# A transformer layer's opening, its gates and its v projections: reordering work around a full TensorE

## The chip, the cores and the metric

One of the cores of a Trainium2 chip runs the whole kernel in one launch. The metric is the device time of one execution in microseconds (us), lower is better. The engines that matter here are TensorE (PE, with its weight loads PEld), VectorE (DVE), ScalarE (ACT), GpSimd (POOL) and SyncE (SP), which issues nearly all transfers.

## The reference, cut to what matters

One layer over 512 tokens of width 1024: a first feed-forward block, a mixer of a chunked mLSTM and a forgetting attention, and a second feed-forward block, each behind an RMS norm that is scaled and shifted by columns computed from a condition vector `c`.

```python
mod = jax.nn.silu(c) @ w_ada + b_ada
sh1, sc1, g1, sh2, sc2, g2, sh3, sc3, g3 = ...
u = rms_norm(x, ffn1_norm_g) * (1 + sc1) + sh1
x = x + 0.5 * g1 * swiglu(u, ffn1_w_in, ffn1_w_out)

u = rms_norm(x, mix_norm_g) * (1 + sc2) + sh2
z = u @ w_mix + b_mix            # q_m k_m v_m o_m i_m f_m q_f k_f v_f f_f g_a g_b
qk_m = jax.nn.silu(causal_conv(jnp.concatenate([q_m, k_m], axis=-1), conv_w, conv_b))
h_m = mlstm_chunkwise(q_m, k_m, v_m, i_m, f_m)
y_a = jax.nn.sigmoid(o_m) * rms_norm(h_m, mlstm_norm_g)
y_b = forgetting_attention(q_f, k_f, v_f, f_f, fox_q_norm_g, fox_k_norm_g)   # 16 heads of 64
merged = jax.nn.sigmoid(g_a) * (y_a @ w_branch_a) + jax.nn.sigmoid(g_b) * (y_b @ w_branch_b)
x = x + g2 * (merged @ w_out)

u = rms_norm(x, ffn2_norm_g) * (1 + sc3) + sh3
x = x + 0.5 * g3 * swiglu(u, ffn2_w_in, ffn2_w_out)
```

All data is float32. The width is 8 blocks of 128 channels, the tokens are 4 blocks of 128.

## The kernel before, in words

**Precision.** Every product is made from rounded high halves and their remainders: a weight is loaded into a `raw` tile (three buffers), `split` (lines 94 to 104) makes its high half `wh` on ScalarE (line 101) and the remainder `wl` on VectorE (line 103), four buffers each. `mm3` (lines 124 to 128) then issues three matmuls, high by high, high by low, low by high. A stationary block is 128x128; the moving side has up to 512 columns. PSUM holds eight banks of 512 columns, four with the tag `g` (`gbank`) and four with the tag `t` (`tbank`).

**Order.** Instructions that are wrapped in `pin` keep the order of the text on their engine. The others are put in order when the kernel is built, by a planner that takes, on each engine, the ready instruction that is first in the text, with its own estimates of when something is ready. On the chip each engine works through its queue in order and waits on semaphores.

**Opening stage** (`start`, lines 693 to 847). The eight channel blocks k of the normalised, scaled input `u` are made one after the other, and each is used at once in 18 matmuls (line 826: three products, six banks). Ahead of block n's use stand: four transposes of the normalised x (`turn(n)`, line 731), the two columns of scale and shift, which VectorE multiplies and adds up from `w_ada` (`mod_first`, `mod`, lines 744 to 752) and TensorE sums over the partitions (`sums(n)`, line 767), two ScalarE instructions on these columns (lines 771, 772), and `uh[n]` and its full value `uf` (lines 773, 775). The low half is a VectorE subtraction (line 777). Block 0's columns come from TensorE directly (`mod0`, line 742). Identity transposes into an unused bank (`fill`, line 726) stand where TensorE waits. In the loop over k, `i` counts the 18 matmuls: before, block 1's transposes are split (two ahead of the loop, two at `i == 7`), its sums stand behind the block after `fill(4)`, and later blocks have transposes at `i == 7` and sums at `i == 12`.

**End of the first FFN** (`end`, lines 1315 to 1396, all pinned). The last banks Z, Y, X, W of the output product are closed, scaled (`scaled`, line 597) and added onto x (`onto`, line 600); x is squared and summed (`x_sq`, line 228). `xnorm` (line 241) turns the sums into a factor per token (`rsqrt`, line 136, a chain of tiny VectorE instructions) and scales x; `norm_turn` transposes (line 295); `u_part` (line 270) makes `u` for half of the tokens. The four first weights of the mixer are split here: `hi(m)` (line 1326) on ScalarE, the function that it returns (line 1328) on VectorE, `lo1`, `lo2`, `lo3` for m = 1, 2, 3. `first(h)` (lines 1380 to 1390) multiplies them with half h of the tokens into four banks `pp[0..3]`, 256 columns at a time.

**Convolutions and gates** (lines 1415 to 1425). `qk_conv(m)` (line 912) takes a bank: a bias copy on ScalarE (line 917), which frees the bank, one and three VectorE instructions (lines 919, 921), Silu (922) and a split (925, 926). `gates` (line 850) projects 280 columns (v of the first four attention heads and the scalar gates) for all tokens in three chunks of weights, 96 matmuls of 280 columns, adds biases (lines 861 to 863), transposes the gates (line 880), and runs a serial chain of Abs, Exp, Ln, scans and Exp (lines 884 to 898). Then channels m = 4 to 7 are projected, one bank and 24 matmuls of 512 columns each.

**Attention heads** (`fox_qkv`, line 1039, and the loop of lines 1462 to 1480). Heads come in four groups g of four. `fox_qkv(g)` projects q and k (512 columns), normalises them, then projects v (256 columns; for g = 0 it is read back from where `gates` put it) and evicts it (`donev`). It is a generator, and so is `gate(m, i)`, a projection of 24 matmuls: the loop over the 16 heads advances them in small steps between the steps of the heads, so that TensorE has work while VectorE and ScalarE run the softmax. `with_gates(gen, n)` appends n gates.

**Ahead of the second FFN** (lines 1515 to 1525) the same `xnorm`, `norm_turn` and `norm_u` (line 299) run twice.

Of the kernel before, what the change touches and what calls it, by code (L numbers as in the profile page):

```python
# [29 lines left out]
BIG = 1e30  # L30
RSQ = (0.2740822732448578, 0.31394892930984497, 0.37500056624412537, 0.4999983012676239, 1.0)

# [14 lines left out]
class Layer:  # L47
# [87 lines left out]

    def rsqrt(self, v, n, pin=lambda i: i):

        nc, sp = self.nc, self.sp
        y = sp.tile([P, n], F32, name=self.nm("rq"), tag=f"rq{n}", bufs=4)
        t = sp.tile([P, n], F32, name=self.nm("rt"), tag=f"rt{n}", bufs=2)  # L140
# [12 lines left out]
        pin(V.scalar_tensor_tensor(y, t, RSQ[4], y, op0=ADD, op1=MUL))  # L153
        return y
# [86 lines left out]
    def xnorm(self, hf, pool):  # L241

        nc, sp = self.nc, self.sp
        v = sp.tile([P, 2], F32, name=self.nm("v"), tag="v", bufs=2)
        s2 = self.ss[:, 2 * hf:2 * hf + 2, :]
        self.pin(nc.vector.tensor_scalar(v, s2[:, :, 0], 1.0 / D, EPS, op0=MUL, op1=ADD))
        self.pin(nc.vector.scalar_tensor_tensor(v, s2[:, :, 1], 1.0 / D, v, op0=MUL, op1=ADD))
        r = self.rsqrt(v, 2, self.pin)
        xn = []
        for i in range(2):  # L250
            x = self.x[2 * hf + i]
            d = self.xn_tiles(pool)
            self.pin(nc.vector.tensor_scalar(d[0], x[0], r[:, i:i + 1], None, op0=MUL))
# [439 lines left out]
    def start(self, st, tp):  # L693
# [16 lines left out]
        def chain(hf):  # L710
            v = sp.tile([P, 2], F32, name=self.nm("v"), tag="v", bufs=2)
            s2 = self.ss[:, 2 * hf:2 * hf + 2, :]
            pin(nc.vector.tensor_scalar(v, s2[:, :, 0], 1.0 / D, EPS, op0=MUL, op1=ADD))
            pin(nc.vector.scalar_tensor_tensor(v, s2[:, :, 1], 1.0 / D, v, op0=MUL, op1=ADD))
            return self.rsqrt(v, 2, pin)
        def norm(tb, h, dve=False):
# [97 lines left out]
        for k in range(NK):  # L814
# [5 lines left out]
            for i, (p, b) in enumerate((p, b) for p in range(3) for b in range(2 * NJ0)):  # L820
                if n < NK and i == 7:
                    turn(n, range(NT) if k else (2, 3))
                if n < NK and k and i == 12:
                    sums(n)
                s = slice(b // 2 * P, (b // 2 + 1) * P)
                pin(nc.tensor.matmul(acc_ps[b], (wl if p == 1 else wh)[:, b % 2, s], self.ul[k] if p == 2 else self.uh[k],  # L826
                                     start=k == 0 and p == 0, stop=k == NK - 1 and p == 2))
# [211 lines left out]
    def fox_qkv(self, g, ip):  # L1039
# [25 lines left out]
        for tb in range(NT):  # L1065
            t3 = tok[tb].rearrange("p (h d) -> p h d", h=8)
            nc.vector.tensor_tensor(t3, t3, r[:, tb * 8:(tb + 1) * 8].unsqueeze(2).to_broadcast([P, 8, 64]), op=MUL)
        bv = self.bias_bcast([(VF + o, 256)], ip) if g else None
        vt = ip.tile([P, NT, 4, P], F32R, name=self.nm("fvt"), tag="vm", bufs=3)
        def donev(tb, ps):  # L1070
            f = ip.tile([P, 256], F32, name=self.nm("vg"), tag="t2", bufs=3)
            if g:
                nc.vector.tensor_tensor(f, ps[:, :256], bv[:, :256], op=ADD)
            else:
                nc.sync.dma_start(f, self.v0_d[tb])
            f4 = f.rearrange("p (h d) -> p h d", h=4)
            nc.scalar.activation(vt[:, tb, :, 0:64], f4, AF.Copy)
            nc.vector.tensor_tensor(vt[:, tb, :, 64:P], f4, vt[:, tb, :, 0:64], op=SUB)
        def mkv(ch):
            def make():  # L1080
                sh = [P, 4, 256]
                r = self.raw(sh, [(lambda t: t, w[ch * 512:(ch + 1) * 512, VF + o:VF + o + 256]
                                   .rearrange("(k p) n -> p k n", p=P))])
                wh, wl = self.split(r, sh)
                return wh, wl, 4 * ch, 4
# [188 lines left out]
    def run(self):  # L1274
# [10 lines left out]
        with tc.tile_pool(name="f1t", bufs=1) as tp:  # L1285
# [5 lines left out]
            with tc.tile_pool(name="f1h", bufs=1) as hp:  # L1291
# [23 lines left out]
                def end(close, scaled, onto):  # L1315
# [110 lines left out]
        with tc.tile_pool(name="att", bufs=1) as ip:  # L1426
# [35 lines left out]
            for n in range(18):  # L1462
                if n % 4 == 0 and n < 16:
                    advance(fill, 99)
                    g = n // 4
                    fill = with_gates(self.fox_qkv(g + 1, ip), 4 if g else 2) if g < 3 else (s for m in range(NK) for s in self.y_a(m, yp, ip))
                last = n >= 12
# [111 lines left out]
```

## Time and profile before

| | |
|---|---|
| median of three runs | 1333.39 us (1333.33 to 1336.34) |
| the profiled execution | 1333.93 us, span 1332.2 us |
| instructions in the span | 18008 |
| busy, share of the span | PE 98%, PEld 82%, DVE 73%, ACT 47%, POOL 3% |
| granted TensorE clock | 1.0 |
| DMA | 254.21 MB, mean 191 GB/s |

Times in rows are us from the span's start. A row of the timeline has start, duration, engine, line, operation, output and inputs, shape, count and, in brackets, how long the engine had been idle before and what ended that. Rows with a count above 1 are merged. A row of the chain has start, duration, engine, output and line. A matmul's duration is its latency; the next one starts earlier.

### The profile page before, as it was taken

Reading aid. Unit: us, or ns where it says so; the run is one execution under the profiler, and the core shown is the slowest. Engines: PE = TensorE matmul, PEld = TensorE weight load, DVE = VectorE, ACT = ScalarE, POOL = GpSimd, SP = SyncE. Lnnn points to the kernel's source line nnn. Section 1 sums busy time; section 2 is a strip of 40 time slices with the busy share of each in tenths; the row PEclk is TensorE's granted clock in tenths of the full one; section 3 lists DMA queues with packets and bytes.
Section 4 is the critical chain, followed back from the end, with each engine's and each line's share of the span. In section 5 each row is a group of like instructions: output and inputs, shape, how many; then the busy total and the mean of one; then the engine's idle time right before and its main releaser. Section 6 shows DMA issues by size and latency. Waiting matters only on the chain.

```text
span 1332.2 us, 18008 instructions
## 1 busy us (share of the span) xinstructions
PE 1311.0 (98%) x6428; PEld 1098.2 (82%) x6428; DVE 966.3 (73%) x1776; ACT 625.0 (47%) x1038; POOL 42.4 (3%) x65
## 2 busy tenths in 40 slices
PE   7999999999999999999999999999999999999998
PEld 6788888878788888888888788778788888888886
DVE  7877777477788687887877778777477656635777
ACT  5533323365476655566666666334253223223742
POOL 1000000000010101000000000003010000000000
PEclk9999999999999999999999999999999999999999
DMA  9999978365835334534252636777529877534574
GB/s 291 276 321 312 317 269 284 113 182 182 280 112 144 108 101 133 159 101 117 65 155 52 181 97 190 217 248 234 163 71 334 282 248 265 201 105 134 172 267 149
DMA packets 205514, 254.21 MB, mean 191 GB/s; under 512 B 15008, under 2 KB 148800, under 8 KB 205424
## 3 DMA queue, kind: packets, MB, share of 16 engines
q1 hardware_dynamic: 205040, 252.98, 60.6%
q8 instruction: 51, 0.84, 0.3%
q14 instruction: 39, 0.32, 0.1%
q0 software_dynamic: 320, 0.06, 0.0%
q10 hardware_dynamic: 64, 0.02, 0.0%
HBM read 217.28 MB, written 35.72 MB: 190 GB/s over the span
## 4 chain that ended last, share of the span: by engine, by line
PE 85%; DVE 7%; DMA 3%; ACT 3%; issue 1%; POOL 0%; ACTq 0%; SPq 0%; DVEq 0%; POOLq 0%
PE g L128 22%; PE g L127 22%; PE g L126 22%; PE t L127 3%; PE t L128 3%; PE t L126 3%; PE g L826 2%; DVE wl L103 2%; PE t L1200 1%; PE t L1170 1%; DMA raw<-in_ffn_w_out_dram 1%; ACT wh L101 1%; PE t L1141 1%; PE t L826 1%; PE t L1142 1%
## 5 line engine op out<-in xcount | busy, mean ns | idle before, releaser
L101 ACT ACTIVATE wh<-raw 128x1024 fp32r<-128x1024 f32 (+2 forms) x250 | 253.8, 1018 | 379.2 <-PE g L127 115.0
L103 DVE TENSOR_TENSOR wl<-raw,wh 128x1024 fp32r<-128x1024 f32 (+2 forms) x250 | 293.4, 1175 | 186.9 <-ACT wh L101 155.6
L127 PE MATMUL g<-ul,wh 128*128 128x512 f32 (+1 forms) x912 | 348.1, 383 | 0.6 <-DVE ul L267 0.3
L126 PE MATMUL g<-uh,wh 128*128 128x512 f32 (+1 forms) x912 | 348.2, 384 | 0.2 <-ACT wh L101 0.2
L128 PE MATMUL g<-uh,wl 128*128 128x512 f32 (+1 forms) x912 | 347.8, 382 | 0.0
L127 PEld LDWEIGHTS g<-ul,wh 128*128 128x128 f32 x912 | 171.3, 188 | 34.0 <-POOL ul L267 1.1
L128 PEld LDWEIGHTS g<-uh,wl 128*128 128x128 f32 x912 | 171.3, 188 | 33.3
L126 PEld LDWEIGHTS g<-uh,wh 128*128 128x128 f32 x912 | 170.8, 188 | 33.0 <-issue 0.6
L126 PE MATMUL g<-wh,uh 128*128 128x512 f32 (+1 forms) x288 | 103.0, 358 | 0.0
L128 PE MATMUL g<-wh,ul 128*128 128x512 f32 (+1 forms) x288 | 102.2, 355 | 0.0
L127 PE MATMUL g<-wl,uh 128*128 128x512 f32 (+1 forms) x288 | 102.0, 354 | 0.0
L325 DVE SCALAR_TENSOR_TENSOR acc<-raw,ccol,acc 128x512 f32<-128x512 f32 (+1 forms) x70 | 66.7, 973 | 30.6 <-DMA raw<-in_w_ada_dram 30.4
L127 PE MATMUL t<-wl,A 128*128 128x512 f32 x176 | 69.2, 393 | 1.1 <-DVE wl L103 1.1
L126 PE MATMUL t<-wh,A 128*128 128x512 f32 x176 | 69.3, 394 | 0.0
L126 PEld LDWEIGHTS g<-wh,uh 128*128 128x128 f32 x288 | 54.3, 189 | 7.7 <-DVE tk L1047 0.5
L128 PEld LDWEIGHTS g<-wh,ul 128*128 128x128 f32 x288 | 54.3, 188 | 7.6
L127 PEld LDWEIGHTS g<-wl,uh 128*128 128x128 f32 x288 | 54.3, 189 | 7.3
L128 PE MATMUL g<-yh,wl 128*128 128x512 f32 x128 | 50.5, 394 | 1.3 <-DVE wl L103 1.3
L127 PE MATMUL g<-yl,wh 128*128 128x512 f32 x128 | 50.2, 393 | 0.0
L126 PE MATMUL g<-yh,wh 128*128 128x512 f32 x128 | 49.9, 390 | 0.0
L455 ACT ACTIVATE A<-E 128x768 fp32r<-128x768 f32 x22 | 18.6, 846 | 55.1 <-DVE E L454 51.0
L1152 ACT ACTIVATE S<-S,mn 128x128 f32<-128x128 f32 (+1 forms) x64 | 35.6, 557 | 17.9 <-DVE mn L1144 9.3
(347 smaller groups left out, 2192.3 us busy)
## 6 DMA issues: line engine op xcount, KB each, us to landing
raw<-in_ffn_w_in_dram SPq DMA_DIRECT2D x82, 512.0 KB
raw<-in_w_ada_dram SPq DMA_DIRECT2D x56, 512.0 KB
raw<-in_w_mix_dram SPq DMA_DIRECT2D x46, 512.0 KB
sa<-in_ffn_w_out_dram SPq DMA_DIRECT2D x22, 512.0 KB
sb<-in_ffn_w_out_dram SPq DMA_DIRECT2D x44, 256.0 KB
ws<-sa SPq DMA_DIRECT2D x22, 512.0 KB
ws<-sb SPq DMA_DIRECT2D x44, 256.0 KB
raw<-ws SPq DMA_DIRECT2D x44, 256.0 KB
```

What stands on the lines that cost most here:

```text
L101: nc.scalar.activation(hi, src, AF.Copy)
L103: self.last_lo = nc.vector.tensor_tensor(lo, src, hi, op=SUB)
L126: pin(mm(ps, lh, rh, start=start, stop=False))
L127: pin(mm(ps, lh, rl, start=False, stop=False))
L128: self.last_mm = pin(mm(ps, ll, rh, start=False, stop=stop))
L325: nc.vector.scalar_tensor_tensor(a, r[:, s], c, a, op0=MUL, op1=ADD)
L455: nc.scalar.activation(A1[:, 0:3, :], E[:, 0:3, :], AF.Copy)
L826: pin(nc.tensor.matmul(acc_ps[b], (wl if p == 1 else wh)[:, b % 2, s], self.ul[k] if p == 2 else self.uh[k], start=k == 0 and p == 0, stop ...
L1141: nc.tensor.matmul(ps[:, :w], q[:, s], k[:, :w], start=True, stop=False)
L1142: nc.tensor.matmul(ps[:, :w], q[:, s], kl[:, :w], start=False, stop=True)
L1152: nc.scalar.activation(S[:, ws], S[:, ws], AF.Exp, scale=-1.0, bias=m, accum_out=sm[:, qb:qb + 1])
L1170: tr = lambda b, c, qb, kb: nc.tensor.transpose(b[:, c:c + P], S[:, P_OFF[qb] + kb * P:P_OFF[qb] + (kb + 1) * P], self.ident)
```

## The change

Six edits.

1. `rsqrt` has 8 VectorE instructions instead of 10 (one for the first guess, the polynomial in two quadratic factors), and the variance ahead of it in the norms over the width takes one instead of two; so 9 instead of 12 there.
2. Opening stage: block 0's two groups of `mod0` matmuls follow each other and its four transposes come behind them; block 1's four transposes all stand at `i == 7` and its sums at `i == 16`, without the fill; later blocks have their sums and right behind them their transposes at `i == 10`.
3. End of the first FFN: `lo2` and `lo3` are made in halves, their second halves after `onto(2, 1, ...)`; one `onto(2, 0, ...)` moves behind `u[7]`.
4. `first(1)` goes over all eight k for channels 0 and 1, then for 2 and 3; `first(0)` stays at k = 0 to 3 and 4 to 7.
5. `gates` stands ahead of the four convolutions in the text.
6. v of head groups 2 and 3 is projected in one product of 512 columns in `fox_qkv(2)`; `fox_qkv(3)` has q and k alone. The numbers of gates behind groups 1, 2, 3 are 2, 2, 6 instead of 2, 4, 4.

```diff
-    def rsqrt(self, v, n, pin=lambda i: i):
+    def rsqrt(self, v, n, pin=lambda i: i, gain=1.0):
...
-        pin(V.tensor_scalar(y.bitcast(I32), v.bitcast(I32), 1, None, op0=ALU.logical_shift_right))
-        pin(V.tensor_scalar(y.bitcast(I32), y.bitcast(I32), -1, 0x5F3759DF, op0=MUL, op1=ADD))
+        s = (gain * RSQ_LEAD) ** 0.25
+        (a0, b0), (a1, b1) = [(a * s, b * s * s) for a, b in RSQ_QUADS]
+        pin(V.tensor_scalar(y.bitcast(I32), v.bitcast(I32), -0.5, 0x5F3759DF, op0=MUL, op1=ADD))
 
         pin(V.tensor_tensor(t, y, y, op=MUL))
-        pin(V.tensor_tensor(t, t, v, op=MUL))
-        pin(V.tensor_scalar(d, t, -1.0, 1.0, op0=MUL, op1=ADD))
-        pin(V.tensor_scalar(t, d, RSQ[0], RSQ[1], op0=MUL, op1=ADD))
-        pin(V.tensor_tensor(t, t, d, op=MUL))
-        pin(V.scalar_tensor_tensor(t, t, RSQ[2], d, op0=ADD, op1=MUL))
-        pin(V.scalar_tensor_tensor(t, t, RSQ[3], d, op0=ADD, op1=MUL))
-        pin(V.scalar_tensor_tensor(y, t, RSQ[4], y, op0=ADD, op1=MUL))
+        pin(V.scalar_tensor_tensor(d, t, -s, v, op0=MUL, op1=MUL))
+        pin(V.tensor_scalar(d, d, s, None, op0=ADD))
+        pin(V.scalar_tensor_tensor(t, d, a0, d, op0=ADD, op1=MUL))
+        pin(V.scalar_tensor_tensor(q, d, a1, d, op0=ADD, op1=MUL))
+        pin(V.scalar_tensor_tensor(y, t, b0, y, op0=ADD, op1=MUL))
+        pin(V.scalar_tensor_tensor(y, q, b1, y, op0=ADD, op1=MUL))
...
-        self.pin(nc.vector.tensor_scalar(v, s2[:, :, 0], 1.0 / D, EPS, op0=MUL, op1=ADD))
-        self.pin(nc.vector.scalar_tensor_tensor(v, s2[:, :, 1], 1.0 / D, v, op0=MUL, op1=ADD))
-        r = self.rsqrt(v, 2, self.pin)
+        self.pin(nc.vector.scalar_tensor_tensor(v, s2[:, :, 0], D * EPS, s2[:, :, 1], op0=ADD, op1=ADD))
+        r = self.rsqrt(v, 2, self.pin, D ** 0.5)
...
         mod0(0)
-        turn(0, (0, 1))
-        turn(1, (0, 1))
         mod0(1)
-        turn(0, (2, 3))
+        turn(0, range(NT))
...
-                if n < NK and i == 7:
-                    turn(n, range(NT) if k else (2, 3))
-                if n < NK and k and i == 12:
+                if n < NK and k == 0 and i == 7:
+                    turn(n, range(NT))
+                if n < NK and i == (10 if k else 16):
                     sums(n)
+                    if k:
+                        turn(n, range(NT))
...
             if n < NK:
-                if k == 0:
-                    fill(4)
-                    sums(n)
                 u_hi(n)
...
-        bv = self.bias_bcast([(VF + o, 256)], ip) if g else None
-        vt = ip.tile([P, NT, 4, P], F32R, name=self.nm("fvt"), tag="vm", bufs=3)
+        if g == 3:
+            self.fx[g] = tok, self.fx[g]
+            return
+        gs = ((0,), (1,), (2, 3))[g]
+        n = len(gs) * 256
+        bv = self.bias_bcast([(VF + o, n)], ip) if g else None
+        vts = [ip.tile([P, NT, 4, P], F32R, name=self.nm("fvt"), tag="vm", bufs=3) for _ in gs]
         def donev(tb, ps):
...
-            f4 = f.rearrange("p (h d) -> p h d", h=4)
-            nc.scalar.activation(vt[:, tb, :, 0:64], f4, AF.Copy)
-            nc.vector.tensor_tensor(vt[:, tb, :, 64:P], f4, vt[:, tb, :, 0:64], op=SUB)
+            for i, vt in enumerate(vts):
+                f4 = f[:, i * 256:(i + 1) * 256].rearrange("p (h d) -> p h d", h=4)
+                nc.scalar.activation(vt[:, tb, :, 0:64], f4, AF.Copy)
+                nc.vector.tensor_tensor(vt[:, tb, :, 64:P], f4, vt[:, tb, :, 0:64], op=SUB)
...
-        self.fx[g] = (tok, vt)
+        self.fx[g] = (tok, vts[0])
+        if len(gs) > 1:
+            self.fx[3] = vts[1]
         if g:
-            yield from self.u_gemm_tokens([mkv(c) for c in range(2)], 256, donev)
+            yield from self.u_gemm_tokens([mkv(c) for c in range(2 * len(gs))], n, donev)
...
                     part(2, 3)
-                    lo2()
                     u[2]()
                     u[3]()
+                    lo2(0, 4)
                     w1 = scaled(W[1], 0)
-                    lo3()
+                    lo3(0, 4)
                     part(4, 5)
                     u[4]()
                     u[5]()
                     onto(2, 1, tx[0, 1])
-                    onto(2, 0, tx[0, 0])
+                    lo2(4, NK)
+                    lo3(4, NK)
                     part(6, 7)
                     u[6]()
                     u[7]()
+                    onto(2, 0, tx[0, 0])
...
-                        for ks in (range(4), range(4, NK)):
+                        for ks in ((range(NK),) if h else (range(4), range(4, NK))):
...
+            columns = self.gates(mp, yp)
             for m in range(4):
                 self.qk_conv(m, self.pp[m], yp, mp)
-            columns = self.gates(mp, yp)
...
-                    fill = with_gates(self.fox_qkv(g + 1, ip), 4 if g else 2) if g < 3 else ...
+                    fill = with_gates(self.fox_qkv(g + 1, ip), (2, 2, 6)[g]) if g < 3 else ...
```

More of the change, by code (lines that the diff above doesn't have):

```diff
@@ L30 @@
 BIG = 1e30
-RSQ = (0.2740822732448578, 0.31394892930984497, 0.37500056624412537, 0.4999983012676239, 1.0)
+RSQ_LEAD = 0.2740822732448578
+RSQ_QUADS = ((-1.0965162378196741, 1.8032570710297795), (2.2419713071789813, 2.0233052502305482))
 QM, KM, VM, OM, IG, FG, QF, KF, VF, FFG, GA, GB = (
@@ L134, in tbank @@
         return self.pt.tile(list(shape), F32, name=self.nm("t"), tag="t")
-    def rsqrt(self, v, n, pin=lambda i: i):
+    def rsqrt(self, v, n, pin=lambda i: i, gain=1.0):
         nc, sp = self.nc, self.sp
         y = sp.tile([P, n], F32, name=self.nm("rq"), tag=f"rq{n}", bufs=4)
-        t = sp.tile([P, n], F32, name=self.nm("rt"), tag=f"rt{n}", bufs=2)
+        t, q = [sp.tile([P, n], F32, name=self.nm("rt"), tag=f"rt{n}", bufs=2) for _ in range(2)]
         d = sp.tile([P, n], F32, name=self.nm("rd"), tag=f"rd{n}", bufs=2)
         V = nc.vector
-        pin(V.tensor_scalar(y.bitcast(I32), v.bitcast(I32), 1, None, op0=ALU.logical_shift_right))
-        pin(V.tensor_scalar(y.bitcast(I32), y.bitcast(I32), -1, 0x5F3759DF, op0=MUL, op1=ADD))
+        s = (gain * RSQ_LEAD) ** 0.25
+        (a0, b0), (a1, b1) = [(a * s, b * s * s) for a, b in RSQ_QUADS]
+        pin(V.tensor_scalar(y.bitcast(I32), v.bitcast(I32), -0.5, 0x5F3759DF, op0=MUL, op1=ADD))
         pin(V.tensor_tensor(t, y, y, op=MUL))
-        pin(V.tensor_tensor(t, t, v, op=MUL))
-        pin(V.tensor_scalar(d, t, -1.0, 1.0, op0=MUL, op1=ADD))
-        pin(V.tensor_scalar(t, d, RSQ[0], RSQ[1], op0=MUL, op1=ADD))
-        pin(V.tensor_tensor(t, t, d, op=MUL))
-        pin(V.scalar_tensor_tensor(t, t, RSQ[2], d, op0=ADD, op1=MUL))
-        pin(V.scalar_tensor_tensor(t, t, RSQ[3], d, op0=ADD, op1=MUL))
-        pin(V.scalar_tensor_tensor(y, t, RSQ[4], y, op0=ADD, op1=MUL))
+        pin(V.scalar_tensor_tensor(d, t, -s, v, op0=MUL, op1=MUL))
[4 more added lines that the diff above has]
+        pin(V.scalar_tensor_tensor(y, q, b1, y, op0=ADD, op1=MUL))
         return y
@@ L712, in chain @@
             s2 = self.ss[:, 2 * hf:2 * hf + 2, :]
-            pin(nc.vector.tensor_scalar(v, s2[:, :, 0], 1.0 / D, EPS, op0=MUL, op1=ADD))
-            pin(nc.vector.scalar_tensor_tensor(v, s2[:, :, 1], 1.0 / D, v, op0=MUL, op1=ADD))
-            return self.rsqrt(v, 2, pin)
+            pin(nc.vector.scalar_tensor_tensor(v, s2[:, :, 0], D * EPS, s2[:, :, 1], op0=ADD, op1=ADD))
+            return self.rsqrt(v, 2, pin, D ** 0.5)
         def norm(tb, h, dve=False):
@@ L1078, in donev @@
-            nc.vector.tensor_tensor(vt[:, tb, :, 64:P], f4, vt[:, tb, :, 0:64], op=SUB)
+            for i, vt in enumerate(vts):
+                f4 = f[:, i * 256:(i + 1) * 256].rearrange("p (h d) -> p h d", h=4)
+                nc.scalar.activation(vt[:, tb, :, 0:64], f4, AF.Copy)
+                nc.vector.tensor_tensor(vt[:, tb, :, 64:P], f4, vt[:, tb, :, 0:64], op=SUB)
         def mkv(ch):
             def make():
-                sh = [P, 4, 256]
-                r = self.raw(sh, [(lambda t: t, w[ch * 512:(ch + 1) * 512, VF + o:VF + o + 256]
+                k = 8 // (2 * len(gs))
+                sh = [P, k, n]
+                r = self.raw(sh, [(lambda t: t, w[ch * k * P:(ch + 1) * k * P, VF + o:VF + o + n]
@@ L1465, in run @@
                     g = n // 4
-                    fill = with_gates(self.fox_qkv(g + 1, ip), 4 if g else 2) if g < 3 else (s for m in range(NK) for s in self.y_a(m, yp, ip))
+                    fill = with_gates(self.fox_qkv(g + 1, ip), (2, 2, 6)[g]) if g < 3 else (s for m in range(NK) for s in self.y_a(m, yp, ip))
                 last = n >= 12
```

6 lines of the change are left out of this document (3 added, 3 removed).

## The prediction

> **What bounds the kernel now.** I read the page's engine line and its chain first, then the busy time by stretches, then the timelines of the stages that the diff touches.
>
> ```profile
> PE 1311.0 (98%) x6428; PEld 1098.2 (82%) x6428; DVE 966.3 (73%) x1776; ACT 625.0 (47%) x1038; POOL 42.4 (3%) x65
> ...
> PE 85%; DVE 7%; DMA 3%; ACT 3%; issue 1%; POOL 0%; ACTq 0%; SPq 0%; DVEq 0%; POOLq 0%
> ```
>
> ```profile
> 300.00:400.00 100.00, 98.57 (x509) 82.67 (x508) 77.75 (x123) 57.01 (x88) 5.21 (x8) 1.00 0.60 191
> 400.00:500.00 100.00, 97.24 (x527) 84.53 (x526) 77.07 (x158) 59.02 (x108) 5.66 (x17) 1.00 0.42 118
> ```
>
> TensorE is the bound: 98% busy, 85% of the chain. So an edit pays only where it takes matmul work away or closes a hole on TensorE; the columns above are span, then PE, PEld, DVE, ACT, POOL busy. The stretch 400:500 holds one hole (2.76 us), 300:400 has 1.43 us. A busy PE still hides waits shorter than a matmul's latency, so I judge by starts, not by busy time. Two pitches are needed:
>
> ```profile
> 59.43 0.39 PE L127 MATMUL g<-ul,wh 128*128 128x512 f32 x1
> ...
> 64.22 0.39 PE L127 MATMUL g<-ul,wh 128*128 128x512 f32 x1
> ```
>
> ```profile
> 642.15 0.28 PE L127 MATMUL g<-wl,uh 128*128 128x256 f32 x1
> ...
> 645.14 0.29 PE L128 MATMUL g<-wh,ul 128*128 128x256 f32 x1
> ```
>
> From the first row to the last are 21 steps in one fence and 25 in the other: 0.2281 us for a 512-column matmul, 0.1196 us for 256 columns, back to back.
>
> **Part A, opening stage.** Timeline, then the chain of waits:
>
> ```profile
> 16.57 0.35 DVE L747 TENSOR_SCALAR ac<-ar,ccol 128x256 f32<-128x256 f32 x1 [0.33 <-DMA ar<-in_w_ada_dram]
> ...
> 19.00 2.04 DVE L752 SCALAR_TENSOR_TENSOR ac<-ar,ccol,ac 128x256 f32<-128x256 f32 x4
> ...
> 23.57 1.20 PE L826 MATMUL g<-uh,wh 128*128 128x512 f32 x4 [1.41 <-ACT uh L773]
> ...
> 25.29 1.00 DVE L752 SCALAR_TENSOR_TENSOR ac<-ar,ccol,ac 128x256 f32<-128x256 f32 x2
> ...
> 30.57 1.00 DVE L752 SCALAR_TENSOR_TENSOR ac<-ar,ccol,ac 128x256 f32<-128x256 f32 x2
> ```
>
> ```profile
> 21.82 0.36 PE t L767 x4
> ...
> 25.45 0.44 PE t L731 x4
> ...
> 27.04 0.34 PE t L767 x4
> 27.38 1.05 PE g L826 x4
> ...
> 28.89 1.09 PE g L826 x4
> ...
> 54.98 1.09 PE g L826 x4
> ```
>
> Block 0: the sums of k=1 stood after the whole block and four filling transposes; now they stand two matmuls before its end. Their input is complete at 19.00+2.04 = 21.04; its start at 16.57 waits for a DMA, so the shorter rsqrt and the regrouped transposes of block 0 can't move it. Sums then run 21.1 to 21.45 instead of 21.82 to 22.18, and block 1 starts 0.73 us earlier. The fill goes; it stood in a wait, so it costs nothing.
>
> Blocks 1 and 2: the sums move from the 13th matmul to the 11th, and all four transposes behind them. TensorE is in order, so everything behind the sums now waits for VectorE's products. These are complete at 25.29+1.00 = 26.29 and 30.57+1.00 = 31.57, and VectorE has no idle time before them that the change takes away. From the start of the sums the rest of the block is 0.34+0.44+8x0.23+0.1 = 2.72 us: the next block starts at 29.05 and 34.3, where it was 28.89 and 34.10. So of the 0.73 all is lost, and 0.2 more.
>
> Blocks 3 to 6: the products are early enough, and TensorE sets the pace. The period was (54.98-28.89)/5 = 5.22. One switch between transposes and matmuls goes (27.38 shows 1.05 where four matmuls need 0.92), and the wait for uh at the block's start goes (28.89: 1.09), because sums and transposes are both over eight matmuls before the end. Period 18x0.228+0.34+0.44+0.12 = 5.02: 0.2 saved four times, 0.8. Part A: -0.6, taken as **-0.5** (bounds: +0.8 if the four blocks also wait for products; -1.6 if all six gain 0.27).
>
> **Part B, end of the first FFN.**
>
> ```profile
> 378.88 0.97 DVE L280 TENSOR_TENSOR ul<-uf,uh 128x256 fp32r<-128x256 f32 x1
> ...
> 383.59 0.41 DVE L280 TENSOR_TENSOR ul<-uf,uh 128x256 fp32r<-128x256 f32 x1
> ...
> 387.87 0.17 DVE L246 TENSOR_SCALAR v<-ss 128x2 f32<-128x2 f32 x1 [0.79 <-ACT rs L228]
> ...
> 390.06 0.16 DVE L153 SCALAR_TENSOR_TENSOR rq<-rt,rq 128x2 f32<-128x2 f32 x1
> ```
>
> ```profile
> 381.63 0.39 PE L1388 MATMUL g<-uh,wl 128*128 128x256 f32 x1 [0.16 <-DVE wl L1328]
> ...
> 390.89 0.30 PE L295 MATMUL t<-ident,xn 128*128 128x128 f32 x1 [0.72 <-DVE xn L253]
> ```
>
> The second normalisation is a chain of 12 tiny VectorE instructions from 387.87 to 390.22, 0.2 us each, and TensorE waits for its end. Now 9: 0.6 us. VectorE's order before it changes too: the low halves of two weights in halves (L1328), so the ul at 378.88 and the matmul at 381.63 come earlier, about 0.5 us on TensorE and 0.4 on VectorE, which was nearly contiguous there. Both reach the transposes about 1.0 earlier: **-1.0**. Weighed against it: the ul at 378.88 took 0.97 where the one at 383.59 took 0.41; the slow one ran beside a GpSimd subtraction. The new order moves other VectorE work to those places; four such meetings stay possible, so by the rows B lies between -1.6 and 0. The Trainium skill's page "SBUF — State Buffer", section "SBUF: two separate sides", calls the shared port an exclusive lock held for the whole instruction: by that rule a VectorE instruction with two SBUF inputs is held up as often in the new order as in the old, and B would be the shorter chain alone, -0.6.
>
> **Part C, gates ahead of the convolutions.**
>
> ```profile
> 402.02 1.27 ACT L917 ACTIVATE cz<-g,colA 128x512 f32<-128x512 f32 x2 [4.66 <-PE g L1390]
> 403.18 2.40 ACT L101 ACTIVATE wh<-raw 128x840 fp32r<-128x840 f32 x3
> ...
> 433.19 0.63 ACT L896 ACTIVATE ggm<-gfs 4x512 f32<-4x512 f32 x1 [1.95 <-DVE gfs L895]
> ```
>
> ```profile
> 402.82 0.55 DVE L919 TENSOR_SCALAR cy<-cz,colA 128x512 f32<-128x512 f32 x1 [4.15 <-ACT cz L917]
> ...
> 407.18 1.02 DVE L103 TENSOR_TENSOR wl<-raw,wh 128x840 fp32r<-128x840 f32 x1
> ...
> 417.38 1.22 DVE L103 TENSOR_TENSOR wl<-raw,wh 128x1024 fp32r<-128x1024 f32 x1
> ```
>
> ```profile
> 404.82 0.68 PE L126 MATMUL t<-wh,uh 128*128 128x280 f32 x4
> 408.26 0.40 PE L127 MATMUL t<-wl,uh 128*128 128x280 f32 x1 [2.76 <-DVE wl L103]
> ...
> 420.41 0.48 PE L126 MATMUL g<-uh,wh 128*128 128x512 f32 x1
> ```
>
> Here is the hole: after four matmuls of the gates TensorE waits 2.9 us for the low half of their weight, because VectorE does two convolutions first (402.82 to 407.18). ScalarE and VectorE sit idle over 4 us before that, since the buffers of four split weights and the first two banks come free only when `first(1)` is nearly over. The change lets `first(1)` finish channels 0 and 1 over all eight k before 2 and 3, so two banks and two weight buffers come free 3 us earlier (half of its 12 us), and puts the gates' splits first. The two splits are then over by about 401 (two each of some 0.8 on ScalarE and 0.95 on VectorE, from 398), where TensorE needs them at 404: **-2.9**. `first(1)` asks for k=4 at 395.7 instead of 398.7; ScalarE and VectorE deliver one k per 0.7 us and I find the last, k=7, needed 0.4 after it is there.
>
> What is queued behind: the convolutions, on ScalarE and VectorE; and behind them the split for m=4 (417.38), which TensorE wanted at 420.41 and now wants at about 416.5. VectorE did 15.8 us of work from 402.82 to its end at 418.6; started at 398.7 it ends at 414.5: 2 us of cover. If VectorE strays by more, the wait comes back there; if all four convolutions start only after the third gates' split, at 404.7, it is 420.5, and C is +1.1. Bounds -2.9 and +1.1. SyncE issues the gates' loads earlier or as before, buffers permitting; GpSimd's memsets there are 0.1 to 0.5 us and nobody's bound.
>
> **Part D, v of head groups 2 and 3 in one product.** 192 matmuls of 256 columns become 96 of 512: 192x0.1196-96x0.2281 = 22.96-21.90: **-1.0** us on a saturated TensorE. By the Trainium skill's page "TensorE: Matmul & The Clock Gate", section "Back-to-back issue gap" (columns/2.4 + 2.5 ns), an estimate is 192x109-96x216 ns, or 0.2 us; the trace's pitches are wider, and decide. The splits, loads and gates per four heads stay six (4+2 and 0+6 for 2+4 twice). VectorE gets 2.8 us more of evictions in heads 4 to 7, less in 8 to 11:
>
> ```profile
> 626.50:663.50 37.00, 36.94 (x229) 32.90 (x228) 28.69 (x80) 22.81 (x47) 0.00 (x0) 1.00 0.23 55
> ```
>
> With 8.3 us of VectorE idle in 37, that is covered on average; a burst at the eviction could cost what it adds, so D lies between -1.0 and +1.8.
>
> **Part E, normalisation ahead of the second FFN.**
>
> ```profile
> 969.98 0.48 DVE L253 TENSOR_SCALAR xn<-x,rq 128x512 f32<-128x512 f32 x1
> ...
> 970.52 0.68 PE L295 MATMUL t<-ident,xn 128*128 128x128 f32 x4
> ...
> 991.58 0.38 PE L127 MATMUL g<-ul,wh 128*128 128x256 f32 x1 [0.31 <-DVE ul L267]
> ```
>
> Both waits hang on the same short chain, two or three instructions of 0.2 us less: 0.3 to 0.4 each, **-0.7** (0 to -1.0). The other rsqrts lie beside matmuls: 0.
>
> **Sum.** -0.5-1.0-2.9-1.0-0.7 = -6.1. The profiled execution took 1333.93 us (span 1332.2), so 1327.8; the median of the runs is 0.54 lower, and so is the forecast: **1327.3 us**.
>
> **Rivals.** (1) The hole moves: m=4's split is late by what the gates gained. For: VectorE has no idle time from 402.82 to 418.6. Against: 2 us of cover. C falls to 0, 1330.2 us, chance 0.18. (2) The queues don't change as the text does: which ready instruction goes first is settled by the planner's times, and the convolutions still stand first. For: in the old order a gates' split already stood between convolutions. Against: first in the text is first among the ready. C and half of B fall: 1330.7, chance 0.1. (3) Slower: on ScalarE the convolutions end up behind the gates' long chain (ending at 433.8, or 429.8 when shifted). Then the third bank, which m=6 needs at 427.5 (416.5 and two products of 24x0.228), comes free after one convolution, about 4 us of hand-overs behind the chain, at some 434.5: 7 us are lost there. And the four convolutions' work, 15.8 us less 3 of the gates' splits, falls into the next stage, where VectorE has 23% to spare: some 4 us more. 1338 us; it decides as soon as the third bank is later than 427.5. Against: in the trace conversions and convolutions slip in between that chain's steps. Chance 0.1.
>
> **Numbers.** Forecast 0.62, rivals 0.18, 0.10, 0.10. About 0.3%, 4 us, can be told from no change: faster (under 1329.4) 0.62, same 0.28, slower 0.10. The range leaves out rival 3 and the sum of the lucky bounds: 1325.0 to 1333.0.
>
> **What would show it.** Right: no wait of the 280-column matmuls for wl; block starts in the opening 5.0 apart from block 3 on, but block 2 later than 28.78; the transposes near 390 without their 0.7 us wait; 96 wide matmuls for v. Wrong: a wait of m=4 for wl, of m=6 for a bank, or new waits of TensorE near heads 6 and 7.

## The result, and the profile after

| | before | after |
|---|---|---|
| median of the runs of one comparison | 1334.39 us (1333.33 to 1336.34, 4 runs) | 1327.84 us (1326.99 to 1328.36, 4 runs) |
| ratio | | 0.995, 95% interval 0.9935 to 0.9964 |
| profiled execution, span | 1332.2 us | 1325.7 us |
| granted TensorE clock | 1.0 | 1.0 |

The forecast was 1327.3 us. The engine line and the chain's shares of the page after:

```profile
PE 1306.7 (99%) x6328; PEld 1090.6 (82%) x6328; DVE 960.1 (72%) x1740; ACT 623.7 (47%) x1038; POOL 42.4 (3%) x65
...
PE 88%; DVE 4%; DMA 3%; ACT 2%; SPq 1%; issue 1%; POOL 0%; ACTq 0%; DVEq 0%; POOLq 0%
```

TensorE has 3 points more of the chain and VectorE 3 fewer: what went was mostly waiting for VectorE. Where it went is told by lengths of stages, each the distance between the starts of two matmuls in the trace:

| stage (us) | before | after | difference |
|---|---|---|---|
| a: from the span's start to the end of the opening | 58.85 | 58.41 | -0.44 |
| b: from there to the first transposes at the first FFN's end | 315.10 | 315.55 | +0.45 |
| c: from `first(0)` to the second transposes | 13.14 | 12.04 | -1.10 |
| d: first 280-column matmul to the first of m=4 | 15.59 | 14.13 | -1.46 |
| e: first to last attention head | 243.97 | 242.67 | -1.30 |
| f: branch products | 90.86 | 88.88 | -1.98 |
| g: w_out to the second transposes ahead of the second FFN | 60.76 | 59.55 | -1.21 |
| h: from there to the last matmul | 338.12 | 338.81 | +0.69 |

Stages a, c, d, e and g are the five terms of the prediction, each with its sign. Its sum was -6.1; the first pair of traces gives -6.5, but with -2.0 in stage f, where the diff changes nothing, and with a smaller d. Stage h isn't touched either: over all profiles of this document it took 337.59 to 339.49 us, so its +0.69 says nothing. The opening, in the chain of waits after:

```profile
20.14 7.04 DMA ar<-in_w_ada_dram
...
30.38 0.60 DVE ul L776
...
31.95 0.61 PE t L766 x4
32.56 0.50 PE t L730 x4
...
37.18 0.34 PE t L766 x4
...
42.15 0.34 PE t L766 x4
...
47.09 0.34 PE t L766 x4
```

The sums at 31.95 hang on VectorE, and through it on a load that took 7.04 us; from 37.18 on sums follow each other at 4.97 and 4.94 us with only TensorE between them. Then the end of the first FFN, VectorE and TensorE:

```profile
387.58 0.16 DVE L247 SCALAR_TENSOR_TENSOR v<-ss 128x2 f32<-128x2 f32 x1 [0.79 <-ACT rs L229]
...
388.57 0.16 DVE L151 SCALAR_TENSOR_TENSOR rt<-rd 128x2 f32<-128x2 f32 x1
388.65 0.15 DVE L152 SCALAR_TENSOR_TENSOR rt<-rd 128x2 f32<-128x2 f32 x1
...
389.16 0.88 DVE L253 TENSOR_SCALAR xn<-x,rq 128x512 f32<-128x512 f32 x2
```

```profile
389.80 2.16 PE L295 MATMUL t<-ident,xn 128*128 128x128 f32 x16 [0.37 <-DVE xn L253]
```

The chain is 1.58 us long, and the wait that was 0.72 is 0.37: shorter, not gone. The gates, ScalarE, VectorE and TensorE:

```profile
398.05 1.70 ACT L102 ACTIVATE wh<-raw 128x840 fp32r<-128x840 f32 x2 [1.79 <-PE g L1397]
...
406.08 1.06 ACT L102 ACTIVATE wh<-raw 128x1024 fp32r<-128x1024 f32 x1 [1.60 <-DMA raw<-in_w_mix_dram]
```

```profile
398.99 1.98 DVE L104 TENSOR_TENSOR wl<-raw,wh 128x840 fp32r<-128x840 f32 x2 [1.48 <-ACT wh L102]
...
412.13 2.73 DVE L917 SCALAR_TENSOR_TENSOR cy<-cz,colA,cy 128x512 f32<-128x512 f32 x4
414.79 1.22 DVE L104 TENSOR_TENSOR wl<-raw,wh 128x1024 fp32r<-128x1024 f32 x1
415.92 0.16 DVE L857 TENSOR_TENSOR gz<-t,bb 128x8 f32<-128x8 f32 x1
```

```profile
404.24 0.30 PE L128 MATMUL t<-wl,uh 128*128 128x280 f32 x1
...
416.09 0.29 PE L129 MATMUL t<-wh,ul 128*128 128x280 f32 x1
416.70 0.29 PE L876 MATMUL t<-ident,gz 128*96 128x128 f32 x1 [0.32 <-PE t L129]
417.30 0.32 PE L876 MATMUL t<-ident,gz 128*96 128x128 f32 x1 [0.32 <-DVE gz L858]
417.79 0.31 PE L876 MATMUL t<-ident,gz 128*96 128x128 f32 x1 [0.17 <-DVE gz L858]
417.86 0.48 PE L127 MATMUL g<-uh,wh 128*128 128x512 f32 x1
```

The two splits start at 398 and the fifth 280-column matmul at 404.24 waits for nothing: the hole is closed. But a new one has opened. From 416.09 to 417.86 are 1.77 us, where before had 0.27: the additions that the gates' transposes need stand on VectorE behind convolutions and a weight's low half.

v, by the groups from the first to the last attention head, first two rows of before, then two of after:

```profile
L126 PE MATMUL g<-wh,uh 128*128 128x512 f32 x96 | 37.8, 394 | 0.0
...
L126 PE MATMUL g<-wh,uh 128*128 128x256 f32 x96 | 27.6, 288 | 0.0
```

```profile
L127 PE MATMUL g<-wh,uh 128*128 128x512 f32 x128 | 50.8, 397 | 0.0
...
L127 PE MATMUL g<-wh,uh 128*128 128x256 f32 x32 | 9.0, 282 | 0.0
```

In each of the three products 64 narrow matmuls became 32 wide ones. No new wait stands near heads 6 and 7.

### The profile page after: what moved, and what is told of

Its sections match the earlier page's. It is cut to its first block, busy times and chain, and to the rows that moved or that the text cites. A ratio compares the mean times of both kernels' runs of the same rounds, so it can differ in the third digit from the quotient of the medians.

```text
span 1325.7 us, 17761 instructions
## 1 busy us (share of the span) xinstructions
PE 1306.7 (99%) x6328; PEld 1090.6 (82%) x6328; DVE 960.1 (72%) x1740; ACT 623.7 (47%) x1038; POOL 42.4 (3%) x65
## 4 chain that ended last, share of the span: by engine, by line
PE 88%; DVE 4%; DMA 3%; ACT 2%; SPq 1%; issue 1%; POOL 0%; ACTq 0%; DVEq 0%; POOLq 0%
PE g L127 23%; PE g L129 23%; PE g L128 23%; PE t L128 4%; PE t L129 4%; PE t L127 4%; PE t L1205 1%; PE t L1175 1%; PE g L825 1%; DVE wl L104 1%; PE t L1146 1%; DMA raw<-in_ffn_w_out_dram 1%; PE t L1147 1%; ACT wh L102 1%; PE t L825 1%
## 5 line engine op out<-in xcount | busy, mean ns | idle before, releaser
L128 PEld LDWEIGHTS g<-ul,wh 128*128 128x128 f32 x912 | 171.3, 188 | 34.3 <-POOL ul L267 1.8
L127 PE MATMUL g<-wh,uh 128*128 128x512 f32 (+1 forms) x256 | 97.4, 380 | 0.0
L129 PE MATMUL g<-wh,ul 128*128 128x512 f32 (+1 forms) x256 | 96.6, 378 | 0.0
L128 PE MATMUL g<-wl,uh 128*128 128x512 f32 (+1 forms) x256 | 96.4, 377 | 0.0
L129 PEld LDWEIGHTS g<-wh,ul 128*128 128x128 f32 x256 | 48.2, 188 | 9.0
L127 PEld LDWEIGHTS g<-wh,uh 128*128 128x128 f32 x256 | 48.2, 188 | 8.7 <-DVE tk L1043 0.5
L128 PEld LDWEIGHTS g<-wl,uh 128*128 128x128 f32 x256 | 48.2, 188 | 8.3
```

Source lines behind the costliest of these rows:

```text
L127: pin(mm(ps, lh, rh, start=start, stop=False))
L128: pin(mm(ps, lh, rl, start=False, stop=False))
L129: self.last_mm = pin(mm(ps, ll, rh, start=False, stop=stop))
```

## The experiments

Runs of one kernel in one comparison spread over 1.1 to 6.1 us, so edits worth less than 1 us aren't told apart by the times. The stage lengths above repeat within 0.2 us in c, e and g, so verdicts go by them, with the time beside. Runs of before in these comparisons had medians of 1335.88, 1335.38 and 1335.15.

My theory after the first pair of traces: the hole needs edits 4 and 5 together; edit 5 gives 1.5 back at the gates' transposes; the first FFN eats the opening's gain; the 2.0 in the branch stage is either the change's or chance.

**1. Convolutions first again.**

```diff
-            columns = self.gates(mp, yp)
             for m in range(4):
                 self.qk_conv(m, self.pp[m], yp, mp)
+            columns = self.gates(mp, yp)
```

> The changed kernel, but with the four convolutions ahead of the gates in the text, as before (edit 5 undone); the new order of first(1) stays. Theory (the new text order closes the hole, and gives 1.5 us back at the gates' transposes): TensorE waits again for the low half of the first gates' weight, 2 to 3 us near 400 to 404, the 1.5 us of waits between the four gates' transposes near 417 go, and the time is 1.2 to 1.5 us above the changed kernel's. Rival 1 (the two are not linked): the hole is back and the transposes still wait, 2.9 us above. Rival 2 (the new order of first(1) alone closes the hole, since two banks and two weight buffers come free earlier for convolutions and gates alike): 0, and the 280-column matmuls wait for nothing.

Measured: 1328.32 us (1326.0 to 1332.0). The first five 280-column matmuls take 0.92 us instead of 0.51, so only 0.4 of the hole is back; the transposes' wait is gone (0.26 from the last 280-column matmul to m=4). My theory falls: rival 2 is right but for 0.4.

**2. The old order of `first(1)`.**

```diff
-                        for ks in ((range(NK),) if h else (range(4), range(4, NK))):
+                        for ks in (range(4), range(4, NK)):
```

> The changed kernel, but first(1) goes over k = 0 to 3 and then 4 to 7 as before (edit 4 undone); the gates stay ahead of the convolutions. Theory (both edits are needed): the first gates' split starts about 3 us later, near 401, its low half is there near 404, the 280-column matmuls wait 0.5 to 1.5 us; time 0.5 to 1.5 us above the changed kernel's. Rival (the text order alone is enough, edit 4 buys nothing): within 0.2 us, no wait there.

Measured: 1328.17 us (1325.16 to 1328.49); 0.51, no wait at all, and 0.37 ahead of m=4. The rival is right: edit 5 alone closes the hole.

**3. v of the groups apart** (the old `fox_qkv`, and `4 if g else 2` gates).

> The changed kernel, but v of head groups 2 and 3 projected apart, 256 columns each, with 2, 4, 4 gates behind the groups (edit 6 undone). Theory of the prediction (only the 96 wide matmuls count): 1.0 to 1.25 us above the changed kernel, all of it between head 7 and the last head; the branch stage stays as in the changed kernel. Rival (the branch stage gained its 2.0 us because the other placing of gates and loads lets the first branch weight be loaded 1.4 us earlier): the waits of 1.0 and 0.7 us for a branch weight's low half come back, 3.0 to 3.3 us above.

Measured: 1329.28 us (1328.87 to 1329.99). Heads first to last 243.93 against 242.67: 1.26, all of stage e. The branch stage is 89.79, not back at 90.86; the theory holds.

**4. The opening in its old order** (`turn`, `mod0`, `sums`, `fill` as before).

> The changed kernel, but with the opening stage's order as before (edit 2 undone; the shorter rsqrt stays). Theory (the opening ends 0.44 us earlier, and the first FFN loses it again because its end hangs on something that doesn't move with TensorE): the transposes near 374 start where they did, time within 0.2 us. Rival (the prediction's part A): 0.4 to 0.5 us above the changed kernel, in every later stage.

Measured: 1328.22 us (1327.25 to 1331.07). The opening ends at 59.14 and the transposes start at 373.91, where the changed kernel had 58.41 and 373.96. By this pair the theory holds; over all profiles only a part of the gain is lost (below, under A), and the time, 0.4 above, can't decide. But this run changed my mind about two other things. Its queues from the first FFN's end on are the changed kernel's, and yet m=4 follows the last 280-column matmul after 0.54 us and not 1.77, and the branch stage takes 90.78 and not 88.88. So I ran the changed kernel again.

**5. The changed kernel again**, nothing edited.

> The changed kernel once more, nothing edited. Theory (TensorE's waits at the gates' transposes and in the branch stage hang on when single weight loads land, which differs from execution to execution with the same queues): from the last 280-column matmul to the first matmul of m=4 it takes anything from 0.5 to 1.8 us (1.77 in the first profile), and moves with the start of ScalarE's split for m=4; from the first branch product to the first product with w_out anything from 88.9 to 91.4 (88.87 in the first profile). Rival (both belong to the change): 1.77 and 88.87 again, within 0.1. Time 1327 to 1329 either way.

Measured: 1328.35 us (1326.38 to 1329.08); 1.32 us ahead of m=4, branch stage 89.79. The rival falls. ScalarE's split for m=4 and the first matmul of m=4 in this run, then the same rows of run 4:

```profile
405.77 1.06 ACT L102 ACTIVATE wh<-raw 128x1024 fp32r<-128x1024 f32 x1 [1.15 <-DMA raw<-in_w_mix_dram]
...
417.54 0.48 PE L127 MATMUL g<-uh,wh 128*128 128x512 f32 x1
```

```profile
404.78 1.06 ACT L102 ACTIVATE wh<-raw 128x1024 fp32r<-128x1024 f32 x1 [0.36 <-DMA raw<-in_w_mix_dram]
...
416.56 0.48 PE L127 MATMUL g<-uh,wh 128*128 128x512 f32 x1
```

The time from issue to landing of that load, in the first profile, in run 5 and in run 4:

```profile
DMA to landing us min/median/max: 6.0/6.0/6.0
```

```profile
DMA to landing us min/median/max: 5.5/5.5/5.5
```

```profile
DMA to landing us min/median/max: 4.7/4.7/4.7
```

Landing 6.0, 5.5, 4.7; split at 406.08, 405.77, 404.78; m=4 at 417.86, 417.54, 416.56, 11.77 or 11.78 behind the split each time. The load, not TensorE, sets when VectorE reaches the additions: the split for m=4 stands ahead of convolutions on ScalarE, its low half ahead of convolutions and additions on VectorE, and all behind it slides. That single loads set the length of the branch stage too is likely, but not shown: the landing is on record for only four or five of its some 30 loads in a profile, and their medians follow the stage loosely (4.3 us where it took 88.88, 5.8 where it took 92.50, but 5.0 where it took 90.78 and 5.4 where it took 89.47).

With before's queues the stage took 90.86, 89.48, 90.31 (before, runs 9 and 10; mean 90.2), with the changed ones 88.88 to 92.50 in ten profiles (mean 90.3). So the -1.98 of the first pair isn't the change's; it is a chance of the two executions.

**6. The additions ahead.**

```diff
             for m in range(4):
-                self.qk_conv(m, self.pp[m], yp, mp)
+                with self.tc.issue_after(self.last_gz.ins) if m > 1 else nullcontext():
+                    self.qk_conv(m, self.pp[m], yp, mp)
```

Here `last_gz` is the last addition to `gz` in `gates`.

> The changed kernel, with the VectorE work of the third and fourth convolution queued behind the last addition that the gates' transposes need. Theory (the additions stand behind convolutions and behind a weight whose load is late, and that is the whole wait): from the last 280-column matmul to the first of m=4 it is 0.3 to 0.4 us whenever the load lands, against 0.5 to 1.8; time 0.2 to 1.4 us below the changed kernel's of the same call. Rival (the work that is put back makes m=5 or m=6 wait, or the heads behind them): the same distance is short, but the first head does not start earlier.

Measured: 1326.36 us (1325.44 to 1327.64), ratio to before 0.9934 (0.9922 to 0.9947); run 5 in the same comparison has 0.9946 (0.9934 to 0.9959). The first addition to `gz` on VectorE, then TensorE's transposes and m=4:

```profile
413.93 0.17 DVE L857 TENSOR_TENSOR gz<-t,bb 128x8 f32<-128x8 f32 x1 [2.05 <-PE t L129]
```

```profile
416.04 0.38 PE L876 MATMUL t<-ident,gz 128*96 128x128 f32 x2
416.18 0.48 PE L127 MATMUL g<-uh,wh 128*128 128x512 f32 x1
```

VectorE now waits for TensorE, and m=4 follows after 0.26 though the load took 5.4 us. From m=4 to the first head it is 133.60 against 133.49 in run 5, so about 0.95 is kept: the theory is right, the rival wrong. By the median this is 2.0 below run 5, more than the theory's 0.2 to 1.4, and below both kernels; the intervals of the two ratios overlap, and the stage, not the time, is what shows it.

**7. The transposes later** (the part of `gates` from the transposes on is called behind m=4's matmuls).

```diff
+                if m == 4:
+                    columns = tail()
                 if m == 7:
```

> The changed kernel, with the gates' transposes and the serial chain behind them after the 24 matmuls of m=4 in the text. Theory: TensorE goes from the last 280-column matmul to m=4 without a wait (0.15 us), 0.4 to 1.6 us less than in the changed kernel, and the chain, 5 us later, still ends before m=7 needs it; time 0.3 to 1.5 us below the changed kernel's of the same call. Rival (the chain now ends too late, at some 436 us, and its columns or the Silu steps of the convolutions that queue behind it on ScalarE are waited for): a wait of 1 to 3 us between m=6 and the first head.

Measured: 1326.92 us (1325.37 to 1327.49). m=4 follows after 0.13 us; from there to the first head it takes 133.78, 0.3 more than in run 5: the four transposes stand there now. No wait of 1 to 3 us: theory right, rival wrong.

**8. The longer rsqrt** (the old `rsqrt` and variance).

> The changed kernel with the longer rsqrt and the two-step variance (edit 1 undone). Theory (12 tiny VectorE instructions of 0.2 us instead of 9 stand alone on the path at three places): from the first 256-column product of the mixer to the second transposes 0.5 to 0.6 us more, and 0.6 more at each of the two waits ahead of the second FFN: 1.8 us above the changed kernel's of the same call. Rival (the prediction's parts B and E: the chain is only part of B, and E is 0.7 in all): 0.6 and 0.7, 1.3 us above. Second rival (edit 3's order made all of B): 0 and 0.7 to 1.2.

Measured: 1330.59 us (1328.14 to 1332.63), 2.24 above run 5. The chain on VectorE, then the second transposes:

```profile
387.72 0.17 DVE L247 TENSOR_SCALAR v<-ss 128x2 f32<-128x2 f32 x1 [0.79 <-ACT rs L229]
...
390.11 0.88 DVE L254 TENSOR_SCALAR xn<-x,rq 128x512 f32<-128x512 f32 x2
```

```profile
390.74 2.16 PE L296 MATMUL t<-ident,xn 128*128 128x128 f32 x16 [1.18 <-DVE xn L254]
```

The chain is 2.39 us instead of 1.58, and TensorE waits 1.18 instead of 0.37: 0.81, and stage c is 0.81 longer. Stage g is 60.74, 1.2 longer: 0.60 at each of its two waits. Edit 1 is worth 2.0 us, more than the theory's 1.8 and far more than the rivals'.

**9. Edit 4 alone, on the kernel before** (the lines of experiment 2, the other way round).

> The kernel before with edit 4 alone: first(1) over all eight k for channels 0 and 1, then 2 and 3. Theory (two causes of the hole, late banks and weight buffers, and the text order; either edit takes most of it): the first four 280-column matmuls are followed by a wait of 0.4 us instead of 2.9; 2.5 us below the kernel before. Rival (in the kernel before, with convolutions first, the gates' splits stay behind them): 2.9 us of wait and the same time.

The first five 280-column matmuls:

```profile
405.88 0.42 PE L126 MATMUL t<-wh,uh 128*128 128x280 f32 x2
406.44 0.40 PE L127 MATMUL t<-wl,uh 128*128 128x280 f32 x1
```

Measured: 1331.26 us (1330.38 to 1332.19), ratio 0.997 (0.996 to 0.9981). Five matmuls take 0.92 us instead of 3.43 and m=4 follows after 0.26: 2.6 gained in stage d. The theory is right there; the median is 3.9 below before's, more than the stage accounts for.

**10. Edit 5 alone, on the kernel before** (experiment 1, the other way round).

> The kernel before with edit 5 alone: the gates ahead of the convolutions in the text. Theory (either edit takes most of the hole): from the first to the fifth 280-column matmul 0.5 to 0.6 us instead of 3.4; the gates' transposes wait 0.1 to 1.5 us; 1.3 to 2.7 us below the kernel before. Rival (edit 5 needs edit 4's earlier buffers): 1 to 2 us of the wait stay. Its branch stage is not touched: if that stage's length hangs on single loads, it is 89 to 92.5 us here, not 90.9 again within 0.1.

Measured: 1332.12 us (1329.38 to 1333.8), ratio 0.9975 (0.9965 to 0.9986). 0.51, then 0.37 ahead of m=4: 2.85 gained in stage d. Branch stage 90.31. The theory is right, and the two edits overlap almost wholly: either takes 2.6 to 2.85, both together 1.5 to 2.7. Some of this is lost again ahead of the first head. From the first 280-column matmul to the first head before took 149.26 us; one edit alone takes 146.75 to 146.92 (runs 1, 2, 9 and 10), both together 146.37 to 147.65 (mean 147.21 of six profiles). So in this stage the second of the two edits bought nothing.

**11. The old order at the end of the first FFN** (`lo2()` and `lo3()` whole, `onto(2, 0, ...)` back).

> The changed kernel with the old order at the end of the first FFN (edit 3 undone: second and third low halves whole, and earlier). Theory (of the 1.1 us between the first 256-column product of the mixer and the second transposes, 0.8 were edit 1's, and 0.3 are left for edit 3): 0.3 us more there, 0.2 to 0.4 us in all. Rival (the prediction's part B, 0.5 for this order): 0.5.

Measured: 1327.63 us (1327.03 to 1329.2). Stage c 12.34 against 12.04: 0.30. The theory is right; the time can't tell it.

**12. Loads of the condition's weights taken earlier** (on top of experiment 6).

```diff
                 last = n >= 12
+                if n % 2 and n < 12:
+                    next(self.ada)
```

> The changed kernel with the additions queued first as in the run before, and six of the loads of the condition's weight matrix that share the three weight buffers with the branch weights taken earlier, one in every second attention head up to the twelfth. Theory (branch weights come late because loads of two kinds share three buffers): the branch stage is 88.9 us, as in the best case, where it was 88.9 to 92.5, and the time 0.5 to 1.5 us below that of the additions alone (1326.4). Rival (the loads and VectorE's products then disturb the heads): the heads take 0.5 to 2 us more, and the sum is 0 or above.

Measured: 1329.98 us (1328.75 to 1331.69). The branch stage is 90.33, no better, and the first seven heads take 113.75 instead of 111.97. TensorE's two long waits there, then VectorE ahead of the second:

```profile
577.24 0.41 PE L1175 MATMUL t<-ident,S 128*128 128x128 f32 x2 [0.85 <-DVE fq L1125]
608.90 0.66 PE L1175 MATMUL t<-ident,S 128*128 128x128 f32 x4 [1.15 <-DVE yb L1209]
```

```profile
605.10 0.69 DVE L1138 TENSOR_TENSOR Am<-A,maskF 128x512 f32<-128x512 f32 x1 [1.80 <-DMA A<-A_d]
```

The rival is right, by both its ways. Behind the first wait stand two of VectorE's products (565.84 and 569.46 in its chain). Behind the second stands a load of the heads, `A`: SyncE issued it at 600.55, where run 6 issued it at 599.50, and it landed 4.46 us later. Why six loads fewer don't shorten the branch stage stays open.

## Why the prediction was right, and where not

**A, -0.5.** The mechanism held: blocks 2 and 3 were forecast to start at 29.05 and 34.3 and did at 29.2 and 34.7. Two sizes were off: block 1 started 0.38 earlier and not 0.73, which the next blocks' waits take back in any case, and the period 5.02 was 4.96. In ten profiles with the new order (the last of them run 12) the opening ends at 57.75 to 58.53 (mean 58.16), in four with the old at 58.85 to 59.60 (59.26): 1.1 earlier. The step not taken was to ask what lies behind it. The first FFN gives some of it back: the transposes at its end start at 373.12 to 374.09 (mean 373.72) against 373.91 to 375.00 (374.41). By these means 0.7 is left, but the ranges overlap, and one pair of traces (58.41 to 373.96, 58.85 to 373.95) shows nothing left. The other 0.4 go at one place, where TensorE waits for the low half of a weight. Its rows, before and after:

```profile
360.93 0.50 PE L127 MATMUL t<-wl,A 128*128 128x512 f32 x1 [0.34 <-DVE wl L103]
```

```profile
360.95 0.50 PE L128 MATMUL t<-wl,A 128*128 128x512 f32 x1 [0.60 <-DVE wl L104]
```

After, TensorE is there 0.24 us earlier, and starts no earlier. From the matmul ahead of this one to its start it takes 0.57 us on average in the four profiles with the old opening and 0.96 in the ten with the new.

**B, -1.0.** Measured 1.10, the parts otherwise than said: 0.81 for the chain (0.6 forecast), 0.30 for the order (0.5). The chain lost three instructions but four steps of 0.2 us: the two factors at 388.57 and 388.65 don't depend on each other and start 0.08 apart, and the step behind them costs what it would cost behind one. By the Trainium skill's page "SBUF — State Buffer", section "SBUF: two separate sides", as weighed in the prediction, the order would have been worth nothing; experiment 11 gives it 0.30. That a slow VectorE instruction with two inputs stands beside one of GpSimd's agrees with the page, in VectorE's rows and GpSimd's of the changed kernel; that the new order has as many of them is the prediction's own step, and the runs don't bear it out:

```profile
379.88 0.41 DVE L280 TENSOR_TENSOR ul<-uf,uh 128x256 fp32r<-128x256 f32 x1
...
382.57 0.96 DVE L280 TENSOR_TENSOR ul<-uf,uh 128x256 fp32r<-128x256 f32 x1
```

```profile
382.17 1.08 POOL L280 TENSOR_TENSOR ul<-uf,uh 128x256 fp32r<-128x256 f32 x1 [0.68 <-ACT uf L277]
```

Before had four that took longer than others of their shape there: two `ul` like the slow one above (at 378.88 and 381.50, 0.97 and 0.96 us), a whole low half (377.19, 1.77 us instead of 1.21) and an addition onto x (383.92, 1.23 instead of 0.68). The changed kernel has three: the `ul` above, another that is slowed by half as much (377.47, 0.69) and a half of a low half (380.82, 1.23 instead of 0.68). Experiment 11, with the old order, has four again.

**C, -2.9.** This term was mis-sized. The hole went, 2.9 us of it. What failed is the step "15.8 us of work ... 2 us of cover": it asked whether the split for m=4 would be late, and it was not; but the gates' own additions stand behind convolutions in the same queue, and m=4's matmuls stand behind the transposes that need them. In six profiles with these queues (after, runs 3, 4, 5, 8, 11) stage d is 12.90 to 14.13, mean 13.69 against 15.59: against the one trace of before, C is -1.9, between -1.5 and -2.7 as one load lands late or early. Rival 1 had the mechanism (the hole moves) with the wrong instruction. The claim that the new order of `first(1)` and the gates' place work together was wrong too: experiments 1, 2, 9 and 10 show each enough alone, and on average no worse than both up to the first head.

**D, -1.0.** Measured 1.30 and, undone, 1.26. The matmuls make 1.06 by the pitches; the other 0.2 wasn't followed up. The prediction's estimate of 0.2 in all used a formula that the Trainium skill's page "TensorE: Matmul & The Clock Gate", section "Back-to-back issue gap", gives for a single matmul by itself and not for a stream; the 1.30 of the trace does not agree with the estimate, and decides.

**E, -0.7.** Mis-sized: 1.21, 0.60 at each wait. The step "two or three instructions of 0.2 us less: 0.3 to 0.4 each" is low by its own figures, which make 0.4 to 0.6. Behind the last wait for ScalarE two instructions went, but three dependent steps: from the second variance instruction to the first scaled x it was 2.19 us before (967.79 to the row at 969.98), eleven steps, and is 1.59, eight:

```profile
967.79 0.16 DVE L247 SCALAR_TENSOR_TENSOR v<-ss,v 128x2 f32<-128x2 f32 x1 [0.85 <-ACT rs L228]
```

```profile
961.82 0.16 DVE L247 SCALAR_TENSOR_TENSOR v<-ss 128x2 f32<-128x2 f32 x1 [0.85 <-ACT rs L229]
...
963.41 0.88 DVE L253 TENSOR_SCALAR xn<-x,rq 128x512 f32<-128x512 f32 x2
```

**Sum.** By these means -0.7, -1.1, -1.9, -1.3 and -1.2 make -6.2, forecast -6.1; the medians differ by 6.55 in the first comparison and by 7.0 (run 5). That the number is so near is luck: C's shortfall of 1.0 met surpluses of 0.1 to 0.5 in each of the others. Rival 2 falls with the rows of the gates' splits; rival 3 would have shown as a longer way from m=4 to the first head, and that took 133.52 us where before took 133.68.

## What to carry to other kernels

When work is put first in an in-order queue, follow everything that the same stage still needs from that queue later, not the first need alone: here a handful of 0.16 us additions behind the displaced work cost up to 1.5 of the 2.9 us. A pair of traces is one draw each: a stage whose first load can land 4.7 or 6.0 us after its issue has to be seen several times before a difference of 1 or 2 us in it is put down to the change. And an edit early in the program keeps only what nothing behind it takes back: here a weight that came no earlier took 0.4 of 1.1 us. Where two edits aim at one hole, each is to be tried alone.

## What was not expected of the hardware

The same load, issued at the same place of the same queues, took 4.7 to 6.0 us to land in five executions, and stage f, in which the diff changes nothing, ranged over 3.6 us between executions. And two VectorE instructions that don't depend on each other started 0.08 us apart where dependent ones of the same size started 0.2 apart, so on these chains the number of dependent steps counted rather than that of instructions.
